# Transposes of the attention's probabilities four steps behind their scaling instead of two, with a fourth buffer

## Chip, cores and metric

The kernel runs on one core of one Trainium2 chip. The metric is the device time of one execution in microseconds (us). The engines are named as the profile names them: PE (TensorE matmuls; PEld is its weight load), DVE (VectorE), ACT (ScalarE), POOL (GpSimd), SP (SyncE, which issues most DMAs).

## What is computed

Two layers of a decoder on 256 tokens of width 2048, all in float32. The first layer mixes tokens by retention, the second by attention in a sliding window, and each is followed by a gated ConvFFN. The change touches the attention alone:

```
proj = h @ w_qkv + b_qkv                      # 32 query heads, 4 key/value heads of 64
scores = einsum(q, k) * dh**-0.5 - slopes * dist      # 128-blocks, window of 128
scores = where(valid, scores, -inf)
probs = softmax(concatenate([scores, sink], -1))[..., :-1]
out = einsum(probs, v)
return out.reshape(B, S, Hq * dh) @ w_out
```

## The kernel before

All large products are done on PE with weights and activations split in two float32r halves, hi and lo. A weight tile arrives by DMA as `raw` (128x2048); ACT copies it to `hi` (L161) and DVE subtracts to get `lo` (L162), in pieces of 1024 columns, so two pieces a tile. PE consumes the tiles one 128-row chunk after the other (L267 and L269 for the query, key and value weights, L256 to L258 for the output weights).

**The order is written out by hand.** `run_main` walks through the weight tiles and counts `self.step`: one step is 512 weight columns of a chunk on PE. A chunk of the queries' weights has 256 columns and is half a step, a chunk of the output weights is one. After every chunk two things are recorded behind it: the next piece of `hi` and `lo`, when the share of the present tile that is done asks for it (`split_ahead`, two pieces in four steps), and then every task that is due (`run_tasks`). A task is a Python generator; the number that it yields is the count of steps until it goes on. Each engine works through its own instructions strictly in the order in which they were recorded, as far as semaphores let it.

**A pair of heads is one task**, `att_pair` (L669). There are 16 pairs, numbered 0 to 15 here, and one begins every four steps. Pairs 0 to 9 follow each other directly; then come about six steps without a new one, and pairs 10 to 15 follow. The parts of a pair, with the step at which they are recorded, counted from the pair's begin:

- 0: the scores, 8 matmuls on PE into two PSUM banks (L684), and the DMA of the position biases `al`;
- 1: maxima on DVE, four reductions that also write `pr` (L692), then two small operations on `soft` (L698, L699);
- 2: exponentials on ACT, four of them in place on `pr` and one on `soft` (L704, L708);
- 4: on DVE the denominators (L710, L711) and the scaling of `pr` (four times L715);
- 6: six transposes of `pr` on PE (L276) into two PSUM banks; ACT copies each bank to the first half of `pT` (L400) and DVE subtracts to get the second (L401);
- 9: the products with the values, 8 matmuls into `po` (L730), and four copies on ACT from `po` to `y` (L739, L740);
- 10: the sum of `y` on DVE (L742), and its halves `yT`: a copy on ACT (L400) and a subtraction on DVE (L401).

The PSUM pool `ms` has four banks, and a pair takes five in its life: two for scores, two for transposes, one for `po`. So a part may also wait for an earlier one to empty its bank. When the weights of a query group are done (every eight steps), `att_queries` adds a copy on ACT (L378), two operations on DVE (L379, L388) and a bias on ACT (L638): called the join here. `pr` has three buffers, `pT` two, `al` two.

The heads' output weights are multiplied in two stages. The first four pairs' share is done while pairs 8 and 9 run; the rest begins during pairs 13 to 15, and its chunk for pair 15 stands at step 32.5 after the begin of pair 10.

Of the kernel before, what the change touches and what calls it, by code (L numbers as in the profile page):

```python
# [9 lines left out]
F32 = mybir.dt.float32  # L10
# [6 lines left out]
P = 128  # L17
# [92 lines left out]
class Kernel:  # L110
# [558 lines left out]
    def att_pair(self, at, qT, i, f):  # L669

        nc = self.nc
        kT, vs = at["kT"], at["vs"]
        jj = f // GRP
        al = self.ph.tile([P, 2, 384], F32, tag="al", name="al", bufs=2)
        nc.sync.dma_start(out=al, in_=self.a["alibi"][f])
        pr = self.ph.tile([P, 2, 384], F32, tag="pr", name="pr", bufs=3)
        soft = self.st.tile([P, 4, NT, 2], F32, tag="soft", name="soft")
        m, nm, es, den = (soft[:, x] for x in range(4))
        pss = [self.ms.tile([P, 512], F32, tag="ms", name="ms") for _ in range(2)]
        where = [slice(0, P), slice(P, P + S)]  # L680
        for t in range(NT):
            for s in range(2):
                rows = slice(s * DH, (s + 1) * DH)
                nc.tensor.matmul(  # L684
                    pss[s][:, where[t]], lhsT=qT[rows, i, t * P : (t + 1) * P],
                    rhs=kT[rows, jj, : (t + 1) * P], start=True, stop=True,
                )
        yield 1
        for s in range(2):
            sink = self.sinks[:, 2 * f + s : 2 * f + s + 1]  # L690
            for t in range(NT):
                nc.vector.tensor_tensor_reduce(  # L692
                    out=pr[:, s, where[t]], in0=pss[s][:, where[t]], in1=al[:, s, where[t]],
                    scale=DH**-0.5, scalar=sink, op0=ALU.add, op1=ALU.max,
                    accum_out=m[:, t, s : s + 1],
                )
        sk = self.sinks[:, 2 * f : 2 * f + 2].unsqueeze(1).broadcast_to([P, NT, 2])
        nc.vector.tensor_scalar_mul(nm, m, -1.0)  # L698
        nc.vector.tensor_tensor(out=es, in0=sk, in1=m, op=ALU.subtract)  # L699
        yield 1  # L700
        for s in range(2):
            for t in range(NT):
                x = pr[:, s, where[t]]
                nc.scalar.activation(  # L704
                    out=x, in_=x, func=AF.Exp, bias=nm[:, t, s : s + 1],
                    accum_out=den[:, t, s : s + 1],
                )
        nc.scalar.activation(out=es, in_=es, func=AF.Exp)  # L708
        yield 2
        nc.vector.tensor_tensor(out=den, in0=den, in1=es, op=ALU.add)  # L710
        nc.vector.reciprocal(den, den)  # L711
        for s in range(2):
            for t in range(NT):
                x = pr[:, s, where[t]]
                nc.vector.tensor_scalar_mul(x, x, den[:, t, s : s + 1])  # L715
        yield 2
        pTs = []
        for s in range(2):
            ps = self.ms.tile([P, 512], F32, tag="ms", name="ms")
            self.transposes(ps, [pr[:, s, n * P : (n + 1) * P] for n in range(3)])  # L720
            pT = self.ph.tile([P, 2, 384], F32R, tag="pT", name="pT", bufs=2)
            self.split_store(pT.unsqueeze(1), ps[:, :384].unsqueeze(1))
            pTs.append(pT)
        yield 3
        po = self.ms.tile([P, 2, S], F32, tag="ms", name="po")
        for s in range(2):
            for m, (q, k) in enumerate(((slice(S), slice(S)), (slice(P, S), slice(S, S + P)))):
                v = vs[:, m, jj, 2 * s : 2 * s + 2].rearrange("p x d -> p (x d)")
                for x in range(2):
                    nc.tensor.matmul(  # L730
                        po[:, s, q], lhsT=v, rhs=pTs[s][:, x, k], start=m == 0 and x == 0,
                        stop=m == 1 and x == 1,
                    )


        y = self.ph.tile([P, 2, S], F32, tag="y", name="y", bufs=2)
        for s in range(2):
            own, other = (slice(DH), slice(DH, P))[:: 1 - 2 * s]
            nc.scalar.copy(out=y[own, 0], in_=po[own, s])  # L739
            nc.scalar.copy(out=y[own, 1], in_=po[other, s])  # L740
        yield 1
        nc.vector.tensor_tensor(out=y[:, 0], in0=y[:, 0], in1=y[:, 1], op=ALU.add)  # L742
        y = y[:, 0]
        self.attT[f] = x = self.ph.tile([P, 2, S], F32R, tag="yT", name="yT", bufs=12)
        self.split_store(x.unsqueeze(1), y.unsqueeze(1))
# [222 lines left out]
```

## Time and profile before

| | |
|---|---|
| median of 3 runs | 2449.4 us (2448.61 to 2450.01) |
| the profiled execution, time | 2448.51 us |
| its span | 2446.4 us |
| PE, DVE, ACT busy | 99%, 64%, 51% of the span |
| attention's pairs | about 1502 to 1683 us from the span's start |

The span runs from the first to the last instruction. A busy time is the sum of an engine's instructions, a wait is idle time of an engine ahead of an instruction, put down to the instruction elsewhere that released it. In the rows of a timeline a bracket shows that idle time and the releaser.

### The profile page before, as it was taken

Reading aid. Unit: us, or ns where it says so; the run is one execution under the profiler, and the core shown is the slowest. Engines: PE = TensorE matmul, PEld = TensorE weight load, DVE = VectorE, ACT = ScalarE, POOL = GpSimd, SP = SyncE. Lnnn points to the kernel's source line nnn. Section 1 sums busy time; section 2 is a strip of 40 time slices with the busy share of each in tenths; the row PEclk is TensorE's granted clock in tenths of the full one; section 3 lists DMA queues with packets and bytes.
Section 4 is the critical chain, followed back from the end, with each engine's and each line's share of the span. In section 5 each row is a group of like instructions: output and inputs, shape, how many; then the busy total and the mean of one; then the engine's idle time right before and its main releaser. Section 6 shows DMA issues by size and latency. Waiting matters only on the chain.

```text
span 2446.4 us, 31283 instructions
## 1 busy us (share of the span) xinstructions
PE 2416.9 (99%) x12612; PEld 2058.9 (84%) x12612; DVE 1561.5 (64%) x2121; ACT 1236.0 (51%) x1815; POOL 29.2 (1%) x37
## 2 busy tenths in 40 slices
PE   8999999999999999999999999899999999999998
PEld 7888888888888888888888888777888888888887
DVE  7555555555556774776577656776677477657774
ACT  6444344344445553555355546766555355535553
POOL 3000000000000000000000000000000000000000
PEclk9999999999999999999999999999999999999999
DMA  7655555555554555555555555344455555555553
GB/s 286 219 184 183 190 184 183 189 185 175 189 189 173 190 189 195 201 186 182 209 181 192 196 188 197 136 153 177 169 195 189 192 201 184 184 209 185 190 200 127
DMA packets 68977, 460.27 MB, mean 188 GB/s; under 512 B 8032, under 2 KB 9184, under 8 KB 16736
## 3 DMA queue, kind: packets, MB, share of 16 engines
q1 hardware_dynamic: 68544, 457.23, 52.7%
q8 instruction: 99, 1.62, 0.3%
q10 hardware_dynamic: 288, 1.05, 0.1%
q14 instruction: 46, 0.38, 0.0%
HBM read 456.15 MB, written 2.10 MB: 187 GB/s over the span
## 4 chain that ended last, share of the span: by engine, by line
PE 92%; DVE 3%; ACT 2%; issue 1%; DMA 1%; POOL 0%; SPq 0%; POOLq 0%; DVEq 0%; ACTq 0%
PE mm L267 32%; PE mm L269 16%; PE mm L256 12%; PE mm L258 12%; PE mm L257 12%; PE po L258 2%; PE po L256 2%; PE po L257 2%; DVE lo L162 1%; PE ms L276 1%; ACT pr L704 1%; PE po L393 1%; ACT hi L161 1%; DVE pr L692 1%; PE ms L503 0%
## 5 line engine op out<-in xcount | busy, mean ns | idle before, releaser
L162 DVE TENSOR_TENSOR lo<-raw,hi 128x1024 fp32r<-128x1024 f32 (+1 forms) x849 | 1018.2, 1218 | 615.4 <-ACT hi L161 614.9
L161 ACT CAST hi<-raw 128x1024 fp32r<-128x1024 f32 (+1 forms) x849 | 857.8, 1042 | 519.7 <-PE mm L258 330.4
L267 PE MATMUL mm<-xT,hi 128*128 128x512 f32 x3552 | 1108.7, 393 | 6.1 <-DVE xT L323 6.1
L269 PEld LDWEIGHTS mm<-xT,lo 128*128 128x128 f32 x3552 | 667.8, 188 | 150.1 <-DVE lo L162 2.6
L269 PE MATMUL mm<-xT,lo 128*128 128x256 f32 x3552 | 702.7, 279 | 0.7 <-DVE lo L162 0.6
L267 PEld LDWEIGHTS mm<-xT,hi 128*128 128x128 f32 x3552 | 541.2, 188 | 11.5 <-ACT hi L161 6.1
L256 PE MATMUL mm<-hi,zT 128*128 128x512 f32 x688 | 268.3, 390 | 0.0
L258 PE MATMUL mm<-hi,zT 128*128 128x512 f32 x688 | 267.7, 389 | 0.0
L257 PE MATMUL mm<-lo,zT 128*128 128x512 f32 x688 | 267.7, 389 | 0.0
L601 DVE SCALAR_TENSOR_TENSOR cv<-u,cw,cv 128x255 f32<-128x255 f32 x344 | 158.3, 481 | 6.1
L256 PE MATMUL mm<-hi,yT 128*128 128x512 f32 x384 | 153.6, 400 | 1.0 <-ACT yT L400 0.9
L258 PEld LDWEIGHTS mm<-hi,zT 128*128 128x128 f32 x688 | 129.1, 188 | 27.0
L256 PEld LDWEIGHTS mm<-hi,zT 128*128 128x128 f32 x688 | 129.1, 188 | 26.5
L257 PEld LDWEIGHTS mm<-lo,zT 128*128 128x128 f32 x688 | 129.2, 188 | 26.4
L257 PE MATMUL mm<-lo,yT 128*128 128x512 f32 x384 | 149.8, 390 | 0.0
L258 PE MATMUL mm<-hi,yT 128*128 128x512 f32 x384 | 149.7, 390 | 0.0
L378 ACT COPY u<-mm 128x512 f32<-128x512 f32 x86 | 50.4, 586 | 183.8 <-PE mm L269 183.8
L379 DVE TENSOR_TENSOR u<-mm,u 128x512 f32<-128x512 f32 x86 | 59.4, 691 | 93.3 <-ACT u L378 93.3
L594 ACT ACTIVATE cv<-u,cw 128x256 f32<-128x256 f32 x172 | 94.2, 595 | 48.6 <-DVE u L388 48.6
L611 ACT CAST zT<-cv 128x256 fp32r<-128x256 f32 x86 | 34.9, 406 | 156.1 <-DVE cv L609 156.1
L256 PE MATMUL mm<-hi,xT 128*128 128x512 f32 (+1 forms) x288 | 109.1, 379 | 0.0
L258 PE MATMUL mm<-hi,xT 128*128 128x512 f32 (+1 forms) x288 | 108.6, 377 | 0.0
(119 smaller groups left out, 1801.1 us busy)
## 6 DMA issues: line engine op xcount, KB each, us to landing
raw<-in_up SPq DMA_DIRECT2D x172, 1024.0 KB, 4.7
raw<-in_ret_in SPq DMA_DIRECT2D x94, 1024.0 KB, 4.7
raw<-in_dn SPq DMA_DIRECT2D x72, 1024.0 KB, 4.8
raw<-in_ret_out SPq DMA_DIRECT2D x32, 1024.0 KB, 4.7
raw<-in_qkv SPq DMA_DIRECT2D x20, 1024.0 KB, 4.7
raw<-in_att_out SPq DMA_DIRECT2D x14, 1024.0 KB, 4.7
raw<-in_dn SPq DMA_DIRECT2D x16, 512.0 KB, 3.3
raw<-in_dn SPq DMA_DIRECT2D x8, 768.0 KB, 4.2
```

The costliest lines, as they stand in the source:

```text
L161: nc.scalar.copy(out=hi, in_=raw)
L162: nc.vector.tensor_tensor(out=lo, in0=raw, in1=hi.bitcast(F32), op=ALU.subtract)
L256: nc.tensor.matmul(out, lhsT=ah, rhs=hi, start=first, stop=False)
L257: nc.tensor.matmul(out, lhsT=ah, rhs=lo, start=False, stop=False)
L258: nc.tensor.matmul(out, lhsT=al, rhs=hi, start=False, stop=last)
L267: nc.tensor.matmul(out, lhsT=hi[:, sl], rhs=both, start=first, stop=False)
L269: nc.tensor.matmul(out[:, :S], lhsT=lo[:, sl], rhs=act[:, 0], start=False, stop=last)
L378: nc.scalar.copy(out=x, in_=g.ps[:, :, S:])
L379: nc.vector.tensor_tensor(out=x, in0=g.ps[:, :, :S], in1=x, op=ALU.add)
L594: nc.scalar.activation(out=c[:, half], in_=u[:, half], func=AF.Identity, scale=w[:, 2:3], bias=w[:, 3:4])
L601: nc.vector.scalar_tensor_tensor(out=c[:, half, d:], in0=u[:, half, : S - d], scalar=w[:, 2 - d : 3 - d], in1=c[:, half, d:], op0=ALU.mult ...
L611: nc.scalar.copy(out=z[:, 0], in_=s)
```

## The change

The yield between scaling and transposes becomes 4, and `pr` gets a fourth buffer. Transposes and the split of `pT` now stand at step 8 of their pair, `po` and the copies to `y` at 11, the sum of `y` and `yT` at 12.

```
-        pr = self.ph.tile([P, 2, 384], F32, tag="pr", name="pr", bufs=3)
+        pr = self.ph.tile([P, 2, 384], F32, tag="pr", name="pr", bufs=4)
...
             for t in range(NT):
                 x = pr[:, s, where[t]]
                 nc.vector.tensor_scalar_mul(x, x, den[:, t, s : s + 1])
-        yield 2
+        yield 4
         pTs = []
         for s in range(2):
             ps = self.ms.tile([P, 512], F32, tag="ms", name="ms")
```

The same instructions are issued, the same DMAs, and the order changes on PE, ACT and DVE. The rows below show one pair's period in the steady part, without a join.

On DVE before, from the end of the maxima to the denominators (`soft` small, `lo` the weights' lower half, `y` the sum, `yT` and `pT` the subtractions):

```order
L698 TENSOR_SCALAR soft<-soft 128x4
L699 TENSOR_TENSOR soft<-sinks,soft 128x4
L162 TENSOR_TENSOR lo<-raw,hi 128x1024
L742 TENSOR_TENSOR y<-y 128x256
L401 TENSOR_TENSOR yT<-y,yT 128x256
L401 TENSOR_TENSOR pT<-ms,pT 128x384 x2
L162 TENSOR_TENSOR lo<-raw,hi 128x1024
L710 TENSOR_TENSOR soft<-soft 128x4
L711 RECIPROCAL soft<-soft 128x4
```

On DVE in the changed kernel, at the same place:

```order
L698 TENSOR_SCALAR soft<-soft 128x4
L699 TENSOR_TENSOR soft<-sinks,soft 128x4
L162 TENSOR_TENSOR lo<-raw,hi 128x1024 x2
L742 TENSOR_TENSOR y<-y 128x256
L401 TENSOR_TENSOR yT<-y,yT 128x256
L401 TENSOR_TENSOR pT<-ms,pT 128x384 x2
L710 TENSOR_TENSOR soft<-soft 128x4
L711 RECIPROCAL soft<-soft 128x4
```

The second piece of `lo`, which stood behind the split of `pT`, now stands ahead of the sum of `y`, and the split of `pT` directly ahead of the denominators.

On ACT before, from the end of one pair's exponentials to the begin of the next pair's:

```order
L708 ACTIVATE soft<-soft 128x4
L161 CAST hi<-raw 128x1024
L739 COPY y<-po 64x256
L740 COPY y<-po 64x256
L739 COPY y<-po 64x256
L740 COPY y<-po 64x256
L161 CAST hi<-raw 128x1024
L400 CAST yT<-y 128x256
L400 CAST pT<-ms 128x384 x2
L704 ACTIVATE pr,soft<-pr,soft 128x128
```

On ACT in the changed kernel:

```order
L708 ACTIVATE soft<-soft 128x4
L739 COPY y<-po 64x256
L740 COPY y<-po 64x256
L739 COPY y<-po 64x256
L740 COPY y<-po 64x256
L161 CAST hi<-raw 128x1024
L400 CAST yT<-y 128x256
L400 CAST pT<-ms 128x384 x2
L161 CAST hi<-raw 128x1024
L704 ACTIVATE pr,soft<-pr,soft 128x128
```

The first piece of `hi` moved from behind the exponentials to behind the copies of `pT`; the copies to `y` now follow the exponentials directly.

On PE in the changed kernel the transposes have moved past four chunks and stand directly ahead of scores, where four chunks (`mm`) stood between them before:

```order
L267 MATMUL mm<-xT,hi 128x512 x2
L269 MATMUL mm<-xT,lo 128x256 x2
L276 MATMUL ms<-ident,pr 128x128 x6
L684 MATMUL ms<-kT,qT 128x128 x2
L684 MATMUL ms<-kT,qT 128x256 x2
```

The scores behind the transposes are those of the pair after next; the second of their two banks is the one that the copies to `y`, recorded one step earlier, empty.

## Rows read from the trace of the kernel before

**Rows 1.** The page: busy time, share of the span, instructions of each engine.

```profile
PE 2416.9 (99%) x12612; PEld 2058.9 (84%) x12612; DVE 1561.5 (64%) x2121; ACT 1236.0 (51%) x1815; POOL 29.2 (1%) x37
```

**Rows 2.** Waits of PE, longest first: us in total, times, longest us.

```profile
PE ms L276 <- DVE pr L715: 12.7, 10, 2.0
```

**Rows 3.** Timeline of one period of pairs: start us, duration us, engine, instruction, count.

```profile
1531.47 0.34 DVE L692 CUSTOM_DVE_ANT_0 pr<-ms,al,sinks 128x128 f32<-128x128 f32 x1
...
1533.10 1.22 DVE L162 TENSOR_TENSOR lo<-raw,hi 128x1024 fp32r<-128x1024 f32 x1
...
1534.23 0.42 DVE L742 TENSOR_TENSOR y<-y 128x256 f32<-128x256 f32 x1
...
1534.74 0.41 ACT L400 CAST yT<-y 128x256 fp32r<-128x256 f32 x1 [2.23 <-DVE y L742]
...
1535.05 0.85 ACT L400 CAST pT<-ms 128x384 fp32r<-128x384 f32 x2
...
1535.55 1.02 DVE L401 TENSOR_TENSOR pT<-ms,pT 128x384 fp32r<-128x384 f32 x2
...
1535.79 0.41 ACT L704 ACTIVATE pr<-pr,soft 128x128 f32<-128x128 f32 x1
...
1537.65 1.04 ACT L161 CAST hi<-raw 128x1024 fp32r<-128x1024 f32 x1
...
1538.59 0.37 ACT L739 COPY y<-po 64x256 f32<-64x256 f32 x1
1538.72 1.22 DVE L162 TENSOR_TENSOR lo<-raw,hi 128x1024 fp32r<-128x1024 f32 x1 [2.15 <-ACT hi L161]
...
1539.87 0.15 DVE L710 TENSOR_TENSOR soft<-soft 128x4 f32<-128x4 f32 x1
...
1540.13 1.05 ACT L161 CAST hi<-raw 128x1024 fp32r<-128x1024 f32 x1
...
1540.70 1.07 PE L276 MATMUL ms<-ident,pr 128*128 128x128 f32 x6 [1.08 <-DVE pr L715]
1541.19 0.35 DVE L692 CUSTOM_DVE_ANT_0 pr<-ms,al,sinks 128x128 f32<-128x128 f32 x1
...
1551.77 0.34 DVE L692 CUSTOM_DVE_ANT_0 pr<-ms,al,sinks 128x128 f32<-128x128 f32 x1
```

**Rows 4.** Timeline of the first pairs, before PE waits.

```profile
1513.07 0.34 DVE L692 CUSTOM_DVE_ANT_0 pr<-ms,al,sinks 128x128 f32<-128x128 f32 x1
...
1514.73 0.40 ACT L704 ACTIVATE pr<-pr,soft 128x128 f32<-128x128 f32 x1 [0.43 <-DVE soft L698]
...
1516.46 0.93 PE L684 MATMUL ms<-kT,qT 64*128 64x128 f32 x8
...
1517.66 1.22 DVE L162 TENSOR_TENSOR lo<-raw,hi 128x1024 fp32r<-128x1024 f32 x1 [0.83 <-ACT hi L161]
...
1524.66 0.93 PE L684 MATMUL ms<-kT,qT 64*128 64x128 f32 x8
```

**Rows 5.** Timeline of the last pairs of both stretches.

```profile
1595.82 0.41 ACT L704 ACTIVATE pr<-pr,soft 128x128 f32<-128x128 f32 x1
...
1600.64 1.16 PE L276 MATMUL ms<-ident,pr 128*128 128x128 f32 x6 [1.97 <-DVE pr L715]
...
1605.76 1.03 PE L730 MATMUL po<-pT,vs 128*128 128x256 f32 x8
...
1636.32 1.23 DVE L162 TENSOR_TENSOR lo<-raw,hi 128x1024 fp32r<-128x1024 f32 x1 [0.83 <-ACT hi L161]
...
1687.59 0.50 PE L256 MATMUL mm<-hi,yT 128*128 128x512 f32 x1 [0.90 <-ACT yT L400]
```

**Rows 6.** PE's timeline; then its windows: length, busy, granted clock, DMA share, GB/s.

```profile
1551.28 1.40 PE L276 MATMUL ms<-ident,pr 128*128 128x128 f32 x6 [1.96 <-DVE pr L715]
...
1552.00:1554.00 2.00, 2.00 (x8) 0.50 0.00 0
1554.00:1556.00 2.00, 2.00 (x9) 0.69 0.25 33
```

More of the change, by code (lines that the diff above doesn't have):

```diff
@@ L675, in att_pair @@
         nc.sync.dma_start(out=al, in_=self.a["alibi"][f])
-        pr = self.ph.tile([P, 2, 384], F32, tag="pr", name="pr", bufs=3)
+        pr = self.ph.tile([P, 2, 384], F32, tag="pr", name="pr", bufs=4)
         soft = self.st.tile([P, 4, NT, 2], F32, tag="soft", name="soft")
@@ L715, in att_pair @@
                 nc.vector.tensor_scalar_mul(x, x, den[:, t, s : s + 1])
-        yield 2
+        yield 4
         pTs = []
```

## The prediction

> **What bounds the kernel now.** I read the page's busy times first: PE is busy for 2416.9 of 2446.4 us, DVE for 64% and ACT for 51% [rows 1]. Over the whole span PE sets the time, so only PE's waits can be won. The list of these waits comes next: 12.7 us, in 10 places, lie ahead of the transposes (L276) until the scaling (L715) is done, at most 2.0 us each [rows 2]. That is the wait at which the change is aimed, and 0.5% of the time. Third I read the timeline of the attention, to see why the scaling is late there. Neither DVE nor ACT is full in that stage: ACT stands idle for 2.23 us ahead of the copy of yT, and DVE for 2.15 us ahead of a piece of lo [rows 3]. They wait for each other.
>
> With L715 of one pair as the starting point, that is a closed loop of things that must follow one another, since each engine keeps its order. Starts in one period [rows 3]: maxima on DVE at 1531.47, a piece of lo at 1533.10, the sum of y at 1534.23, ACT's copy of yT at 1534.74, pT at 1535.05, the exponentials at 1535.79, a piece of hi at 1537.65, its lo on DVE at 1538.72, the denominators at 1539.87, the next pair's maxima at 1541.19. The links are 1.63 + 1.13 + 0.51 + 0.31 + 0.74 + 1.86 + 1.07 + 1.15 + 1.32 = 9.72 us. PE needs less for a pair: from one pair's scores at 1516.46 to the next's at 1524.66, where it didn't wait, 8.20 us [rows 4]. So in this stage the loop through ACT and DVE sets the pace, and PE's wait at the transposes is where that shows. A period with a join is longer: 1541.19 to 1551.77 is 10.58 us, 0.86 more [rows 3].
>
> **What the change does to that loop.** It adds no instruction and no DMA; six transposes, two copies on ACT and two subtractions on DVE move by two steps, and with them everything behind them in the pair: po, four copies to y, the sum, the halves of yT. SP's queue keeps its order. The fourth buffer of pr is no work, and pr is written again only three pairs later; I cost it at nothing.
>
> The transposes themselves get four steps of slack instead of two, and the exponentials no longer stand behind the copies of pT on ACT. But by the order the engines now form another loop, and it has to be summed from the same rows. On ACT the copies to y follow the exponentials, then a piece of hi, then yT and pT. On DVE the lo of that piece stands ahead of the sum of y, and the subtractions for pT stand ahead of the denominators. Link by link:
>
> - maxima to exponentials 1.66 (1513.07 to 1514.73, where ACT waited for just that) [rows 4];
> - exponentials to what ACT does next 1.86 (1535.79 to 1537.65);
> - copies to y 1.54 (1538.59 to 1540.13);
> - hi to its lo 1.07 (1537.65 to 1538.72);
> - lo to the sum of y 1.13 (1533.10 to 1534.23);
> - sum to ACT's yT 0.51, yT to pT 0.31 (1534.23, 1534.74, 1535.05);
> - pT to DVE's first subtraction 0.50 (1535.05 to 1535.55), both subtractions 1.02;
> - denominators to the next maxima 1.32 (1539.87 to 1541.19) [rows 3].
>
> The sum is 10.92 us, 1.20 more than the 9.72 of before: the copies to y and the subtractions come into the loop (2.56, and 0.03 and 0.50 - 0.74 of other differences), and one lo goes out of it (1.15). With a join I add the same 0.86, since L378, L379 and L388 stand between the copies to y and lo as they stood between exponentials and lo: 11.78. Where blocks of output weights end, DVE also adds to the residual there; that falls into the time in which it waits for hi.
>
> PE then waits elsewhere. The second bank of the scores (for the later pairs, of the transposes) is the one that po had, and it is free when the copies to y of one step before are done. That is 1.86 + 1.54 = 3.40 us after the exponentials begin, once a period, so PE's wait per pair becomes 10.92 - 8.20 = 2.7 us, or 3.6 with a join, instead of 1.5 and 2.4 by the same reckoning.
>
> **First stretch, pairs 0 to 9.** Up to the exponentials of pair 1 at 1514.73 nothing changes. Their hi ends in the lo at 1517.66 [rows 4], which now is followed by pT, denominators and maxima: 1517.66 + 1.13 + 1.02 + 1.32 + 1.66 = 1522.79 for the exponentials of pair 2. Seven periods later, three of them with a join, those of pair 9 begin at 1522.79 + 4 x 10.92 + 3 x 11.78 = 1601.81; before they began at 1595.82 [rows 5], so 6.0 us later. At the end the products of pair 8 wait for pT, which DVE begins 1.86 + 1.54 + 1.07 + 1.13 + 0.51 + 0.31 + 0.50 = 6.92 us after these exponentials and ends 1.02 later, at 1609.75. Then PE has half of po (0.5), one step, transposes (1.07), three steps and po of pair 9 (1.03). A step is about 1.35: 8.20 less 0.93, 1.07 and about 0.8 of the attention's own matmuls, over four. That makes 1617.75. Before, po of pair 9 ended at 1606.79 [rows 5], two steps earlier in PE's order, so 1609.5 at the same point. The stretch loses 8.3 us.
>
> **Second stretch, pairs 10 to 15**, on the old time scale. The lo at 1636.32 [rows 5] gives the exponentials of pair 12 at 1636.32 + 5.13 = 1641.45, of pair 15 one period with a join and two without later: 1675.07. DVE's pT for pair 14 is done at 1675.07 + 7.94 = 1683.01, and PE is through po of pair 15 some 8 us later (half of po, a step, transposes, three steps, po): 1691.0. Then the chunk for pair 15 stands a single step behind, where before there were three, and needs copies to y, hi, lo, sum and the copy of yT itself: 1.54 + 1.07 + 1.13 + 0.51 + 0.41, 1695.7. Before it began at 1687.59, after a wait of 0.90 us for the same tile [rows 5]. The stretch loses 8.1 us. Behind it everything is as before, and PE has no wait that could give it back.
>
> **The clock.** After a wait of 1.96 us at 1551.28 PE was granted 0.50 of its clock from 1552 to 1554 and 0.69 from 1554 to 1556, which is 1.2 GHz for a part of it, and costs about 1.0 + 0.6 us; after the equal wait of 1.97 us at 1600.64 it was not [rows 5, 6]. The new waits are longer. Inside the loop a loss of 1.6 us on PE lies beside its 2.7 us of waiting and costs nothing. At the three waits that end the stretches (po of pair 8, po of pair 14, the chunk for pair 15; about 3 us each) it counts in full: 0 to 4.8 us. I take one of three, 1.6 us, since one of the two longest waits before had it.
>
> **Sum.** 8.3 + 8.1 + 1.6 = 18.0 us. The profiled execution took 2448.5 (span 2446.4), so 2466.5 for its like; on the median of 2449.4 it is 2467.4. I predict 2467.
>
> **Rivals.**
> - *The wait simply goes.* If the pace were PE's own 8.20 us a pair, the 12.7 us would be won: 2436.7. The Trainium skill speaks for it: "Perfetto Trace Analysis", section "Optimization Strategy", says that the same gap repeating on the engine that should be full can mean too few buffers for the next tile. The gap does repeat here, 10 times; but ACT's 2.23 us in the loop are a wait for DVE's sum, not for a buffer [rows 3]. This rival holds if DVE were not kept behind hi by its lo, so that the sum of y came early. 5%.
> - *The wait only changes its place.* If the loop kept its 9.72, PE would wait as long at the scores as now at the transposes: 2449 to 2453. This needs a slack of 1.2 us in my links, for instance pieces of hi done well ahead of the copies to y. 7%.
> - *Half of the loss*, one stretch alone or 0.6 us a period: 2457 to 2458. 5%.
> - *The clock falls after each of the long waits*: three instead of one, 2449.4 + 16.4 + 4.8 = 2470.6. The Trainium skill bears on it: "TensorE: Matmul & The Clock Gate", section "HAM oscillation — how this bites in real kernels", tells of a matmul loop that falls back to the half clock at every wait. By that rule the time is this rival's; the trace shows it at one wait of two so far. 20%.
>
> The forecast itself keeps 63%. Slower by more than 0.2%, which is about what can be told from no change here (5 us): the forecast, the clock and half of the loss, 88%; the second rival 7%, the first 5%. The range leaves out these two: from 2456, half of the loss, to 2472, the clock's case with a little more in the links. One mechanism would end above it: a half clock that stays through the loops. PE would then need up to twice 8.20 us a pair, past 10.92; the dip before lasted less than 4 us, and I leave it out.
>
> **What would show it.** Right: in the steady part exponentials begin 10.9 and 11.8 us apart; PE's list has L276 waiting for L715 gone, and in its place waits of 2 to 4 us a pair at L684 and L276 until ACT's L740; ACT goes from L704 straight into L739; DVE waits more than 2 us ahead of a lo until hi, with the sum of y behind it; a wait of 2 us or more ahead of L256 until yT. Wrong: starts of the exponentials 8.2 us apart (the first rival) or 9.7 (the second), or the loss in waits at L267 and L269 for lo, which I expect to have none.

## The result and the profile after

The changed kernel takes 2470.28 us (median of 4 runs, 2467.20 to 2470.94); the kernel before, beside it, 2449.67 us. The ratio is 1.0082, with a 95% interval from 1.0065 to 1.0100: 20.6 us slower. The forecast was 2467, in a range from 2456 to 2472. The profiled execution took 2470.94 us with a span of 2468.8, against 2448.51 and 2446.4 before.

First the page of the changed kernel (busy us, share of the span, instructions), which answers to [rows 1]:

```profile
PE 2428.4 (98%) x12612; PEld 2070.5 (84%) x12612; DVE 1561.8 (63%) x2121; ACT 1237.1 (50%) x1815; POOL 29.2 (1%) x37
```

The instructions are as many as before, and DVE and ACT work as long as before. PE is busy for 11.5 us longer with the same matmuls. Its waits answer to [rows 2] (us in total, times, longest us):

```profile
PE ms L276 <- ACT y L740: 7.9, 4, 2.8
PE ms L684 <- ACT y L740: 7.4, 4, 3.0
...
PE po L730 <- ACT pT L400: 5.3, 2, 2.7
PE mm L256 <- ACT yT L400: 3.6, 1, 3.6
PE mm L269 <- DVE lo L162: 0.9, 2, 0.5
```

The 12.7 us at the transposes for L715 are gone, as the change means them to be. In their place stand 7.9 + 7.4 us for the bank that the copies to `y` empty, 5.3 us for `pT` and 3.6 us for `yT` of the last pair. Where did the 22.4 us of span come from? PE's list adds up to 31.8 us with the lines not shown (among them 6.1 us for `xT`, the same in both kernels and outside the attention), against 20.7 before: 11.1 us. With 11.5 us more of busy PE that is 22.6, so the account closes. It says where PE's time lies, not what sets it. The longer busy time has its place as well; these are windows of PE in the changed kernel, behind the wait for `pT` of pair 8 (length, busy, granted clock, DMA share, GB/s):

```profile
1610.00:1612.00 2.00, 1.99 (x9) 0.50 0.00 0
...
1614.00:1616.00 2.00, 2.00 (x10) 0.50 0.76 229
1616.00:1618.00 2.00, 2.00 (x11) 0.89 0.70 295
```

A granted clock of 0.50 is 1.2 GHz. Adding up 1 less the clock, times 2 us, over the windows from 1520 to 1716 us gives 15.4 us; before it was 1.7, nearly all of it in [rows 6]. Of the 15.4 us, 8.5 lie inside the two stretches, behind four waits of 2.83 to 3.04 us, and 6.8 behind the three waits at their ends: 3.4 behind the one for pair 8 (the windows above), 1.7 behind each of the other two.

The pace of the loop is read from the timeline of ACT and DVE, which answers to [rows 3]. This is one period without a join in the changed kernel (start us, duration us, engine, instruction, count, and in brackets the idle time before and its releaser):

```profile
1558.47 0.40 ACT L704 ACTIVATE pr<-pr,soft 128x128 f32<-128x128 f32 x1 [1.85 <-DVE soft L698]
...
1560.34 0.35 ACT L739 COPY y<-po 64x256 f32<-64x256 f32 x1
...
1561.86 1.04 ACT L161 CAST hi<-raw 128x1024 fp32r<-128x1024 f32 x1
1561.89 1.65 PE L684 MATMUL ms<-kT,qT 64*128 64x128 f32 x6 [3.04 <-ACT y L740]
...
1562.93 1.22 DVE L162 TENSOR_TENSOR lo<-raw,hi 128x1024 fp32r<-128x1024 f32 x1 [3.30 <-ACT hi L161]
...
1564.08 0.42 DVE L742 TENSOR_TENSOR y<-y 128x256 f32<-128x256 f32 x1
...
1564.59 0.40 ACT L400 CAST yT<-y 128x256 fp32r<-128x256 f32 x1 [1.68 <-DVE y L742]
...
1564.90 0.86 ACT L400 CAST pT<-ms 128x384 fp32r<-128x384 f32 x2
...
1565.40 1.02 DVE L401 TENSOR_TENSOR pT<-ms,pT 128x384 fp32r<-128x384 f32 x2
...
1566.34 0.15 DVE L710 TENSOR_TENSOR soft<-soft 128x4 f32<-128x4 f32 x1
...
1567.66 0.34 DVE L692 CUSTOM_DVE_ANT_0 pr<-ms,al,sinks 128x128 f32<-128x128 f32 x1
...
1569.34 0.40 ACT L704 ACTIVATE pr<-pr,soft 128x128 f32<-128x128 f32 x1 [2.64 <-DVE soft L698]
```

Read it as a ring: DVE waits 3.30 us for `hi`, which stands behind the four copies to `y`; ACT waits 1.68 us for DVE's sum, and 2.64 us for DVE's maxima (through `soft`). The period is 1569.34 - 1558.47 = 10.87 us. The one before it, with a join, began at 1546.73 and was 11.74. PE's 3.04 us at the scores is where this shows; PE delays nobody in this ring.

### The profile page after: what moved, and what is told of

The parts are those of the page before. It is cut to its first block, busy times and chain, and to the rows that moved or that the text cites. A ratio compares the mean times of both kernels' runs of the same rounds, so it can differ in the third digit from the quotient of the medians.

```text
span 2468.8 us, 31277 instructions
## 1 busy us (share of the span) xinstructions
PE 2428.4 (98%) x12612; PEld 2070.5 (84%) x12612; DVE 1561.8 (63%) x2121; ACT 1237.1 (50%) x1815; POOL 29.2 (1%) x37
## 4 chain that ended last, share of the span: by engine, by line
PE 91%; DVE 4%; ACT 3%; issue 1%; DMA 1%; POOL 0%; SPq 0%; POOLq 0%; DVEq 0%; ACTq 0%
PE mm L267 31%; PE mm L269 16%; PE mm L256 12%; PE mm L257 12%; PE mm L258 12%; PE po L256 2%; PE po L258 2%; PE po L257 2%; DVE lo L162 1%; ACT pr L704 1%; PE ms L276 1%; DVE pr L692 1%; PE po L393 1%; ACT hi L161 1%; DVE pr L715 1%
## 5 line engine op out<-in xcount | busy, mean ns | idle before, releaser
L267 PE MATMUL mm<-xT,hi 128*128 128x512 f32 x3552 | 1111.5, 394 | 6.1 <-DVE xT L323 6.1
L269 PEld LDWEIGHTS mm<-xT,lo 128*128 128x128 f32 x3552 | 669.9, 189 | 150.4 <-DVE lo L162 2.0
L269 PE MATMUL mm<-xT,lo 128*128 128x256 f32 x3552 | 703.7, 280 | 0.9 <-DVE lo L162 0.9
L267 PEld LDWEIGHTS mm<-xT,hi 128*128 128x128 f32 x3552 | 542.9, 189 | 12.2 <-ACT hi L161 6.3
L256 PE MATMUL mm<-hi,zT 128*128 128x512 f32 x688 | 268.3, 390 | 0.0
L256 PE MATMUL mm<-hi,yT 128*128 128x512 f32 x384 | 155.1, 404 | 3.6 <-ACT yT L400 3.6
L256 PEld LDWEIGHTS mm<-hi,zT 128*128 128x128 f32 x688 | 129.1, 188 | 26.5
L256 PE MATMUL mm<-hi,xT 128*128 128x512 f32 (+1 forms) x288 | 109.1, 379 | 0.0
```

Source lines behind the costliest of these rows:

```text
L256: nc.tensor.matmul(out, lhsT=ah, rhs=hi, start=first, stop=False)
L267: nc.tensor.matmul(out, lhsT=hi[:, sl], rhs=both, start=first, stop=False)
L269: nc.tensor.matmul(out[:, :S], lhsT=lo[:, sl], rhs=act[:, 0], start=False, stop=last)
```

## Experiments

The theory: the new order closes a longer loop through ACT and DVE (10.9 and 11.8 us a pair, PE needs 8.20), and two rest terms come with it, the ends of the two stretches and the clock. Rivals are the fourth buffer, the PSUM bank at which PE waits, and the clock. Each of the runs below was timed in 3 rounds, with the kernel before beside it.

**One part alone.** First the distance without the buffer, on the changed kernel:

```
-        pr = self.ph.tile([P, 2, 384], F32, tag="pr", name="pr", bufs=4)
+        pr = self.ph.tile([P, 2, 384], F32, tag="pr", name="pr", bufs=3)
```

> Four steps between scaling and transposes, but three buffers for pr as before: the one half of the change alone. Loop theory (the order on ACT and DVE sets a period of 10.9 us, 11.7 with a join): the buffer is no part of the loop, so the time is that of the changed kernel, 2470, within 3 us. Rival that the fourth buffer costs something (other addresses, other waits): nearer to 2449.7. Rival that three buffers are too few at this distance: above 2473, with waits of DVE's maxima for the transposes.

Measured: 2468.85 us, ratio 1.0077 (1.0062 to 1.0092). Then the buffer without the distance, on the kernel before:

```
-        pr = self.ph.tile([P, 2, 384], F32, tag="pr", name="pr", bufs=3)
+        pr = self.ph.tile([P, 2, 384], F32, tag="pr", name="pr", bufs=4)
```

> Two steps as before, with the fourth buffer: the other half of the change alone. Loop theory: the order is that of the kernel before, 9.72 us a period, so 2449.7 within 2 us. Rival that the buffer matters: over 2 us away from it.

Measured: 2449.81 us, ratio 1.0000 (0.9990 to 1.0009). Its waits at the transposes for L715 stay as they were, 13.9 us in 11 places. So the effect is that of the distance, and the buffer changes nothing in either order that these times could show.

**A distance between.** In the changed kernel:

```
-        yield 4
+        yield 3
```

> Three steps between scaling and transposes, four buffers. Loop theory: with this distance the copies to y stand ahead of the exponentials on ACT, and yT, pT and their subtractions between the exponentials and the next denominators. The loop is maxima, exponentials, yT, pT, hi, lo, denominators: 1.66 + 1.86 + 0.31 + 0.74 + 1.07 + 1.15 + 1.32 = 8.11 us, below PE's 8.20 a pair, and about 9.0 with a join. PE's waits ahead of the transposes go and do not come back at the banks: 2438 to 2444, faster than both kernels, with a wait of about 2 us left at the chunk for pair 15 (its yT comes one step later). Rival (the more steps, the longer a bank is held, and PE waits for banks; the order does not matter): between the two kernels, 2455 to 2465.

Measured: 2435.47 us, ratio 0.9941 (0.9926 to 0.9956), faster than both kernels and than expected. Exponentials and copies on ACT with three steps:

```profile
1549.27 0.40 ACT L704 ACTIVATE pr<-pr,soft 128x128 f32<-128x128 f32 x1 [0.77 <-DVE soft L698]
...
1551.13 0.39 ACT L400 CAST yT<-y 128x256 fp32r<-128x256 f32 x1
...
1555.11 0.36 ACT L739 COPY y<-po 64x256 f32<-64x256 f32 x1 [0.94 <-PE po L730]
...
1557.40 0.40 ACT L704 ACTIVATE pr<-pr,soft 128x128 f32<-128x128 f32 x1 [0.79 <-DVE soft L698]
```

The copies to `y` now stand ahead of the exponentials instead of behind them, and ACT reaches them early enough to wait 0.94 us for PE. The sum finds its copies done, and `yT` follows the exponentials at once. The period is 8.13 us (9.06 with a join), about PE's own 8.20. PE's waits in the attention, but for three of 0.2 us:

```profile
PE mm L256 <- ACT yT L400: 2.0, 1, 2.0
PE ms L276 <- DVE soft L692: 1.6, 3, 0.6
```

Two, three and four steps give 2449.7, 2435.5 and 2470.3 us: more slack between two operations doesn't make the time go one way. What counts is which instructions the order puts into the ring.

**A link taken out.** In the changed kernel, the sum of `y` goes from DVE to POOL:

```
-        nc.vector.tensor_tensor(out=y[:, 0], in0=y[:, 0], in1=y[:, 1], op=ALU.add)
+        nc.gpsimd.tensor_tensor(out=y[:, 0], in0=y[:, 0], in1=y[:, 1], op=ALU.add)
```

> The changed kernel with the sum of y on POOL instead of DVE; nothing else moves. Loop theory: ACT's copy of yT no longer waits behind DVE's lo. The loop is then exponentials 1.86, copies to y 1.54, hi to lo 1.07, lo 1.13, subtractions for yT and pT 0.38 + 1.02, denominators to maxima 1.32, maxima to exponentials 1.66: 9.98 us (10.8 with a join) instead of 10.87. About 0.9 us in each of 10 periods and in both tails, so 2456 to 2462. Rival (PE waits for the bank that the copies to y empty, whatever DVE does): 2470 within 3 us, since the copies to y stand where they stood. Rival that the period cannot be moved by one link: also 2470.

Measured: 2451.43 us, ratio 1.0005 (0.9995 to 1.0015). The rows of one period, with POOL:

```profile
1553.33 0.40 ACT L704 ACTIVATE pr<-pr,soft 128x128 f32<-128x128 f32 x1 [3.01 <-DVE soft L698]
...
1556.71 1.05 ACT L161 CAST hi<-raw 128x1024 fp32r<-128x1024 f32 x1
1556.74 1.15 PE L684 MATMUL ms<-kT,qT 64*128 64x128 f32 x6 [2.05 <-ACT y L740]
1556.76 0.73 POOL L742 TENSOR_TENSOR y<-y 128x256 f32<-128x256 f32 x1 [10.01 <-ACT y L740]
...
1557.79 1.23 DVE L162 TENSOR_TENSOR lo<-raw,hi 128x1024 fp32r<-128x1024 f32 x1 [3.29 <-ACT hi L161]
...
1559.27 1.02 DVE L401 TENSOR_TENSOR pT<-ms,pT 128x384 fp32r<-128x384 f32 x2
...
1563.20 0.41 ACT L704 ACTIVATE pr<-pr,soft 128x128 f32<-128x128 f32 x1 [3.43 <-DVE soft L698]
```

From the start of `lo` to that of the subtraction for `pT` there are now 1.48 us (1557.79 to 1559.27), where the changed kernel has 2.47 (1562.93 to 1565.40), and the period is shorter by just this: 9.87. The bank is emptied as long after the exponentials as before (1553.33 to 1556.71, 3.38 us; above 1558.47 to 1561.86, 3.39), and PE still waits for it, but 2.05 us instead of 3.04. Hence the bank is not what sets the pace. The period came out 0.1 us shorter than expected and the time 5 us below: the ring is passed thirteen times (ten periods and the three waits at the ends), and 13 times 1.0 are 13 us of the 18.9 against the changed kernel's 2470.28. Most of the rest is the clock. From the first exponentials to the chunk for pair 15 this trace has 183.43 us instead of 201.91, 18.5 less: 10.0 in the ten periods and 8.5 at the ends. The clock stayed at 1.00 behind the products of pairs 8 and 14 here, where its fall costs the changed kernel 4.4 us (the run with filled waits below); with the 3 us of the ring that is 7.4 of the 8.5. The clock's loss over the attention is 5.2 us instead of 15.4.

**Work put into the ring, and beside it.** Four copies whose results nobody reads, on ACT, once behind the copies to `y`, once behind the copies of `pT`:

```
+        extra = self.st.tile([P, 4, P], F32, tag="sq", name="sq", bufs=2)
+        for i in range(4):
+            nc.scalar.copy(out=extra[:, i], in_=self.ident)
```

> The changed kernel with four extra copies on ACT (the identity, 128x128, to a scratch tile that nobody reads) in each pair, directly behind the copies to y. The bank of po is empty before them, as without them. An ACT operation of 128x128 took about 0.3 us start to start, so 1.2 us a pair. Loop theory: they lie in the loop, so the period grows from 10.87 to about 12.0 us, and by the same in both tails: 13 times 1.2, 2480 to 2488. Rival (PE waits for the bank that the copies to y empty, and nothing else sets the pace): 2470 within 3 us.

> The changed kernel with the same four extra copies on ACT in each pair, but directly behind the copies of pT, where ACT later waits 1.85 to 2.64 us for the maxima. Loop theory: they fit into that wait and are no part of the loop: period 10.87 and 11.74 as without them, 2470 within 3 us. Rival (ACT simply has too much to do in this stage): as much slower as with the copies in the other place, 2480 to 2488.

Measured: 2480.34 us in the ring, ratio 1.0125 (1.0110 to 1.0140), and 2468.75 beside it, ratio 1.0077 (1.0060 to 1.0094). Here is ACT in the first of them:

```profile
1560.15 0.40 ACT L704 ACTIVATE pr<-pr,soft 128x128 f32<-128x128 f32 x1 [1.85 <-DVE soft L698]
...
1563.53 0.90 ACT L743 COPY sq<-ident 128x128 f32<-128x128 f32 x4
1564.34 1.04 ACT L161 CAST hi<-raw 128x1024 fp32r<-128x1024 f32 x1
...
1571.82 0.40 ACT L704 ACTIVATE pr<-pr,soft 128x128 f32<-128x128 f32 x1 [2.65 <-DVE soft L698]
```

And in the second:

```profile
1558.53 0.40 ACT L704 ACTIVATE pr<-pr,soft 128x128 f32<-128x128 f32 x1 [1.05 <-DVE soft L698]
...
1565.69 0.90 ACT L726 COPY sq<-ident 128x128 f32<-128x128 f32 x4
...
1569.39 0.40 ACT L704 ACTIVATE pr<-pr,soft 128x128 f32<-128x128 f32 x1 [1.85 <-DVE soft L698]
```

The same 0.80 us of ACT make a period of 11.67 in one place and leave it at 10.86 in the other, where ACT's idle time ahead of the exponentials takes them up (1.85 instead of 2.64). Thirteen times 0.80 are 10.4 us. From the first exponentials to the chunk for pair 15 the traces have 210.66 and 200.25 us, which is 10.4; the medians lie 11.6 apart, and the first is 10.1 above the changed kernel's. I had expected 1.2 a period, since I priced a copy at 0.3 us and it takes 0.20. This is the run that shows the ring most plainly: the same work on the same engine costs everything or nothing, by its place in the order.

**The link taken out of the kernel before.** The same edit of L742 with two steps and three buffers, and with three steps and four buffers:

> The kernel before (two steps, three buffers) with the sum of y on POOL. Loop theory: without DVE's sum ACT's copy of yT need not wait behind maxima and lo, and the longest loop left is maxima to exponentials 1.66, exponentials to hi 1.86, hi to lo 1.07, lo 1.15, denominators 1.32: 7.06 us (7.9 with a join), below PE's 8.20. The 12.7 us of waits at the transposes go: 2436 to 2441. Rival (two steps are too few for the transposes, whatever stands in the queues): 2446 to 2450, the waits stay.

> Three steps, four buffers, and the sum of y on POOL. Loop theory: three steps alone already leave PE's own pace, so little is left to win: the wait at the chunk for pair 15 (2.0 us) gets shorter, by up to 1 us, and 1.6 us of waits for DVE's maxima may go. 2433 to 2436. Rival that every link taken from DVE helps by its length: 2430 or less.

Measured: 2430.87 us with two steps, ratio 0.9924 (0.9909 to 0.9939), and 2431.43 with three, ratio 0.9925 (0.9911 to 0.9940). Both beat both kernels. The second is 1.6 us below its expectation: against three steps alone, the wait at the chunk for pair 15 goes from 2.0 to 0.2 us, and with it the only half clock that three steps left (1.7 us, behind that wait). With two steps, all that is left of PE's waits in the attention is this:

```profile
PE ms L276 <- DVE soft L692: 1.3, 2, 0.6
```

So the 12.7 us of before were to be had by breaking the ring, with no more time for the transposes. The gain, 18.7 us, is above the 9 to 14 expected. Its span is 18.2 shorter: PE's waits are 12.9 less (7.8 in all), and PE's busy time 5.1 less. Of these 5.1, 1.7 is the half clock of [rows 6], which is gone; the rest I have not itemised.

**The clock at the last waits.** Twelve matmuls (128x512 each) that write into the empty `po`, ahead of the products of pairs 8 and 14; the products then overwrite them:

```
+        if f in (8, 14):
+            self.fill(po.rearrange("p s q -> p (s q)"), vs)
```

> The changed kernel with twelve matmuls more (128x512, about 0.22 us each, their result overwritten by the real products) ahead of the products with the values of pairs 8 and 14, where PE waits 2.7 us for pT and its clock falls to half behind. They fill that wait with work. If the half clock behind these waits is what lengthens the ends of the two stretches, it stays away there, po of pair 8 to po of pair 9 takes about 8.5 us instead of 10.54, po of pair 14 to po of pair 15 about 8.3 instead of 9.26, and the kernel takes 3 us less: 2466 to 2468 beside 2470. Rival (the clock is no part of the time, the ends are longer for another reason): 2470 or, by the work added, up to 2475.

And as a control the same matmuls into the first bank of the scores of pairs 3 to 7, so inside the ring, and the changed kernel once more beside them:

> The changed kernel with the same twelve matmuls ahead of the scores of pairs 3 to 7, where PE waits up to 3.0 us for the copies to y and its clock falls behind the wait. Loop theory: PE's half clock is hidden there, since the loop through ACT and DVE sets the pace; the clock stays up, the exponentials still begin 10.87 and 11.74 us apart, and the time is that of the changed kernel, 2470 within 2 us. Rival (the falling clock inside the stretch is what the change costs): 5 us less or more, 2465 and below.

> The changed kernel once more, on the same chip as the two with more matmuls, for their comparison: 2470 within 2 us.

Measured: 2466.76, 2468.71 and 2467.87 us, ratios 1.0068 (1.0053 to 1.0084), 1.0078 (1.0063 to 1.0093) and 1.0073 (1.0056 to 1.0090). In these times the first effect is only 1.1 us, within what separates two timings of the changed kernel (2470.28 and 2467.87). The traces tell it apart. First PE in the changed kernel, at the products of pairs 8, 9, 14 and 15 and the chunk for pair 15:

```profile
1609.78 2.35 PE L730 MATMUL po<-pT,vs 128*128 128x256 f32 x8 [2.66 <-ACT pT L400]
...
1620.32 1.03 PE L730 MATMUL po<-pT,vs 128*128 128x256 f32 x8
...
1693.64 0.38 PE L730 MATMUL po<-pT,vs 128*128 128x256 f32 x1 [2.67 <-ACT pT L400]
...
1702.90 1.03 PE L730 MATMUL po<-pT,vs 128*128 128x256 f32 x8
...
1708.99 0.80 PE L256 MATMUL mm<-hi,yT 128*128 128x512 f32 x1 [3.62 <-ACT yT L400]
```

The same with the filled waits (L673 are the fillers, L738 is the former L730):

```profile
1606.71 2.88 PE L673 MATMUL po<-xT,vs 128*128 128x512 f32 x12
1609.55 0.39 PE L738 MATMUL po<-pT,vs 128*128 128x256 f32 x1
...
1617.28 1.03 PE L738 MATMUL po<-pT,vs 128*128 128x256 f32 x8
...
1690.58 0.39 PE L738 MATMUL po<-pT,vs 128*128 128x256 f32 x1
...
1698.27 1.03 PE L738 MATMUL po<-pT,vs 128*128 128x256 f32 x8
...
1704.48 0.79 PE L256 MATMUL mm<-hi,yT 128*128 128x512 f32 x1 [3.75 <-ACT yT L400]
```

And a window of it, where the changed kernel had 0.50 (length, busy, granted clock, DMA share, GB/s):

```profile
1610.00:1612.00 2.00, 1.86 (x13) 1.00 0.00 0
```

With PE kept at work the clock stays at 1.00 (2.4 GHz) there, and from the products of pair 8 to those of pair 9 it is 7.73 us instead of 10.54, from pair 14 to 15 7.69 instead of 9.26 (the second timing of the changed kernel has the same 10.54 and 9.26; expected were 8.5 and 8.3). The fillers delay nothing: the products of pair 8 begin 102.67 us after the first exponentials with them, 102.70 without. So the half clock cost 2.8 and 1.6 us at these two waits.

The first of them cost more because it got more of it. In the run with three buffers the same wait for pair 8 (2.67 us) was followed by this, where the changed kernel has 0.50 in three windows:

```profile
1612.00:1614.00 2.00, 2.00 (x9) 0.50 0.15 33
1614.00:1616.00 2.00, 2.00 (x12) 0.76 0.83 311
```

Its loss of clock is 1.7 us instead of 3.4, and from pair 8 to 9 it needs 9.29 us instead of 10.54, 1.6 more than with the filled wait. The run with copies beside the ring has 1.7 us and 9.30, the control below and the second timing of the changed kernel 3.4 us and 10.42 and 10.54.

The profiled executions show the effect once the start of the attention is taken out: they differ by 2.85 us (2469.35 and 2466.50), and the filled one began its attention 1.33 us later (1506.88 and 1505.55 for the first exponentials); together that is the 4.2 us of the stage. Why the medians lie only 1.1 us apart stays open; what the half clock costs is therefore read from the traces alone.

In the control the clock stays up at the filled pairs, inside the ring. A window of PE in the changed kernel, inside the ring:

```profile
1542.00:1544.00 2.00, 2.00 (x8) 0.50 0.12 47
```

The same window in the control:

```profile
1542.00:1544.00 2.00, 2.00 (x14) 1.00 0.02 4
```

Yet the control's exponentials begin at 1545.87, 1557.62 and 1568.49, still 11.75 and 10.87 us apart. Inside the ring the half clock costs nothing, since PE has the time. So of the changed kernel's falls only those at the ends count.

## Why the prediction was right, and where it was off

**The bound.** That ACT and DVE set the pace and not PE is borne out by the two orders that shorten their ring: with three steps, and with the sum on POOL in the kernel before, the pace becomes PE's own.

**The links.** The ten links of the period shown above, in the prediction's order, with the predicted value in brackets: maxima to exponentials 1.68 (1.66), exponentials to the copies 1.87 (1.86), copies 1.52 (1.54), `hi` to `lo` 1.07 (1.07), `lo` to the sum 1.15 (1.13), sum to `yT` 0.51 (0.51), `yT` to `pT` 0.31 (0.31), `pT` to the subtractions 0.50 (0.50), subtractions 0.94 (1.02), denominators to maxima 1.32 (1.32). The sum is 10.87 (10.92), and with a join 11.74 (11.78). All durations came from the trace of before; only their neighbours changed. That is why a ring that no trace had shown could be summed.

**The place of the waits** came as forecast, at L684 and L276 for L740, with two more at L730 and one at L256; there was none of size at L267 and L269 for `lo` (0.9 us). They don't come at every pair, as "2 to 4 us a pair" had it. Four waits have 2.83 to 3.04 us, where 3.6 were reckoned for a period with a join; the other periods show 1.3 us or less. Behind each of the four PE ran at half clock and took longer over its own work, which fits that little or nothing was left to wait for in the next period; this was not tested apart.

**The two stretches.** In the changed kernel the exponentials of pair 0 begin at 1507.08, where before it was 1505.72; this offset of 1.36 us is there from the first scores on and differs from run to run, so I take it out. From these exponentials to the chunk for pair 15 the changed kernel needs 1708.99 - 1507.08 = 201.91 us, against 1687.59 - 1505.72 = 181.87 before [rows 5]: 20.0 more. With the two waits filled it is 1704.48 - 1506.88 = 197.60, so 15.7 us without the half clock. The prediction had 8.3 + 8.1 = 16.4. Split at the exponentials of pair 10 (1624.37 before, 1636.16, and 1633.13 with the filled waits), the first stretch lost 10.4 us and the second 9.6, without the half clock 7.6 and 8.1: the first term was 0.7 too large, the second exact.

**The clock is the mis-sized term.** The prediction took "one of three, 1.6 us", since before one wait of 2 us out of two had been followed by the half clock [rows 5, 6]. It followed all three waits, and cost 2.8 + 1.6 = 4.4 at the first two (20.0 less 15.7 is 4.3), and some 1.0 us behind the third: by the transposes at the end of the attention the delay has grown from 20.0 to 21.05 us. That is 5.3 instead of 1.6. So against the forecast's 18.0 us, the 22.4 of the span have 3.7 more from the clock, 0.7 less from the first stretch, and 1.4 from the later start of the attention, which no term foresaw and which goes either way from run to run.

The rival "the clock falls after each of the long waits" is what happened, and its 2470.6 is nearer to the 2470.28 than the forecast. Its 4.8 came near as a sum only: one wait cost 2.8, more than the 1.6 read from before, since the half clock lasted longer there (3.4 us lost instead of 1.7), and one 1.0. That a fall counts by its place shows in the kernel before as well: with the fourth buffer the one fall came behind the wait at 1601.74 us, at the end of the first stretch, and the products of pairs 8 and 9 lay 11.18 us apart instead of 9.74. Over the three other runs with the same ring and waits (buffer undone, copies beside the ring, the same kernel again) the medians were 2468.85, 2468.75 and 2467.87, between the forecast and this rival, so the times alone don't choose between the two; the traces do.

The Trainium skill, "TensorE: Matmul & The Clock Gate", section "HAM oscillation — how this bites in real kernels", tells of a matmul loop that falls back to the half clock at every one of its waits. The trace agrees with that for these three waits, of 2.66, 2.67 and 3.62 us, and for the four of 2.83 to 3.04 us in the ring; it does not for the ring's three waits of 0.95 to 1.30 us, and before, the wait of 1.96 us was followed by half clock and the one of 1.97 us was not [rows 5, 6].

**The other rivals.** "The wait simply goes" fails, and with it what was cited for it from the Trainium skill, "Perfetto Trace Analysis", section "Optimization Strategy", that a repeating gap can mean too few buffers: with a fourth buffer and the old distance nothing changes (2449.81), and with three and the new one the loss stays (2468.85). "The wait only changes its place" needed 1.2 us of slack in the links, and there was none. "Half of the loss" fails too, since both stretches lost.

## What to carry to other kernels

Where an engine waits at the same place in every period, sum the ring that the other engines form before giving the waiting instruction more slack: start at one instruction, go from each to the next that must follow it, by data or by the order on its engine, and compare the sum with the bound engine's own work per period. Then write down the order after the change and sum the new ring from the same rows; a distance moves everything recorded behind it, and a short link taken out of the ring (0.73 us on an idle POOL) won 18.7 us here with no more slack at all. Price waits of the matmul engine that nothing behind can give back, at the ends of such a stretch, with the half clock that follows them.

## What the runs showed of the hardware

- What the half clock cost was unequal after nearly equal waits: 2.66 us of waiting were followed by 2.8 us of loss, 2.67 by 1.6 us. Behind one and the same wait (pair 8, 2.66 to 2.68 us) the clock lost 3.4 us in three runs and 1.7 in two.
- Twelve matmuls ahead of the wait kept the clock at 1.00 for 2.88 us of work that nobody reads; standing in the place of a wait of 2.66 us they made the stage behind it shorter, 7.73 us instead of 10.54.
- POOL's sum of 128x256 took 0.73 us, where DVE's row shows 0.42, and was still the better place, since POOL had nothing queued ahead of it.
- A copy of 128x128 on ACT added 0.20 us to the ring; the first such row shows 0.90 us for four, and the next instruction began 0.81 us after their begin. Instructions of one engine overlap a little, so a ring is summed from starts, not from durations.
